# Copies and additions of weight sums spread over the projection tiles of a decoder block, and a later load of token blocks

## The chip, the core and the metric

The kernel runs on one NeuronCore of a Trainium2 chip. The core's engines work side by side, each through its own list of instructions in order: TensorE (PE in the profile, with its weight loads as PEld), VectorE (DVE), ScalarE (ACT), GpSimd (POOL) and SyncE (SP), which here only issues DMA transfers. Sixteen DMA engines carry the transfers of all queues. The metric is the device time of one launch in microseconds, the median of several runs.

## What is computed

One decoder block over 1040 positions (16 learned meta tokens and 1024 tokens) of width 1024, in float32:

```python
h = layer_norm(concat(meta, x))
p = h @ w_in + b_in            # u_s5 | q | k | v | o | i | f | g_s5 | g_m
y_s5 = glu(gelu(s5(u_s5)) @ s5_w_glu)                  # grouped diagonal state-space model
y_m  = (sigmoid(o) * head_norm(mlstm(silu(conv(q, k)), v, i, f))) @ m_w_out   # 4 heads
mix  = sigmoid(g_s5) * y_s5 + sigmoid(g_m) * y_m
h = layer_norm(alpha * h + mix @ w_o)
h = layer_norm(alpha * h + relu(h @ w_up + b_up)**2 @ w_down)
out = h[:, 16:]
```

## The kernel before

A float32 product is made of three matmuls over operands that are split into a high and a low part (`mm3`, L226 to L228). ACT writes the high part (`whi`, L212) and DVE the low part (`wlo`, L213).

**Stages.** The start (`ln0_pipe`) normalises nine blocks of x, transposes them on PE (L1259) and makes the first four projection tiles; `hT_hi` and `hT_lo` are the split result, and `h_dr` a copy of it in DRAM. Then 42 weight tiles ("jobs") follow, one after the other: `ORDER` lists 30 of them, and a q stands for a q and a k tile, so that tiles 0 to 33 are projections (tile 4 is `v0`, tile 5 the k or q behind it); tiles 34 to 41 are `z0` to `z7`, the tiles of the gated S5 product. Beside them generators in "lanes" run the convolutions, the four mLSTM heads, S5, and at the end `ah_scale` and `up_early`, which prepare later stages (`wpre` tiles, stored to `wu_dr`). A clock of estimated times decides when a lane's next piece is written into the program; a scheduler then orders each engine's list by its own simulated times.

**The first mLSTM head.** `gates` transposes the gate values on PE (tiles `gps`, L375 to L421), stores two rows to DRAM (`grow_dr`, L411, and `wrow_dr`), and each head loads them back spread over all partitions (`gB`, `wiB`, L426 and L428). DVE and ACT turn `gB` into weights (L444, L448), ACT makes `kw` (L460), and PE multiplies (`pu`, L477).

**Seven products.** Behind the tiles, `Seven` computes six gate tiles and the mLSTM's output projection with seven products for a 2 x 2 block of tiles instead of eight. It needs sums of weight blocks, made ahead of it in DRAM by `w_sums`: `ws_dr[p, 0..3]` for three pairs of tiles of `wf` and four of `wmo`. Each transfer covers all pairs of one kind (3 x 256 KB or 4 x 256 KB); GpSimd issues it, and an addition (`accum_op`) adds the source to what stands in DRAM. The lane `ws` issues 11 for each weight, one per 6 us of the estimated clock, from the end of the start on. `Seven` also needs sums of token blocks: `begin` loads four raw blocks (`rawb`, two transfers each) from `h_dr`, and `first` loads its first weights, splits them, and subtracts the blocks (L1000). `begin` is called ahead of `z6`, `first` ahead of `z7`, and `run7` behind all tiles.

**Buffers.** Weights, sums, raw blocks and most temporaries share 30 buffers (`slot`); a new tile waits for the release of the buffer that it takes. SP issues weight loads two tiles ahead of their use (`load_w`, L198).

Of the kernel before, what the change touches and what calls it, by code (L numbers as in the profile page):

```python
# [9 lines left out]
F32 = mybir.dt.float32  # L10
# [3 lines left out]
OP = mybir.AluOpType  # L14
# [19 lines left out]
JU, JQ, JK, JO, JGS, JGM = 0, 4, 8, 12, 20, 28  # L34
# [8 lines left out]
NM = 2  # L43
# [69 lines left out]
def decoder_block(  # L113
# [5 lines left out]
    v_, a_, g_, t_ = nc.vector, nc.scalar, nc.gpsimd, nc.tensor  # L119
    const = ctx.enter_context(tc.tile_pool(name="const", bufs=1, side="left"))  # L120
# [17 lines left out]
    def f32(ap):  # L138
        return ap.bitcast(F32)
# [4 lines left out]
    lanes = {"ml": Lane(), "cv": Lane(), "s5": Lane(), "s5c": Lane(), "s5g": Lane(), "ah": Lane()}  # L144
# [49 lines left out]
    def load_w(job):  # L194
        job.raw = []
        for src, n in job.loads:
            r = slot("wraw") if ring[0] is None else ring[0].tile([P, 1024], F32, tag="wr", bufs=3, name="wraw")
            nc.sync.dma_start(r[:, :n], src)  # L198
            job.raw.append(r)

    def split_w(job, later=False):
        if later:
            return split_now(job, True)
        with tc.high_priority(offset=SPLIT_UP):
            split_now(job)
# [26 lines left out]
    def next_split(jobs, i):  # L232
        if i + 1 < len(jobs) and jobs[i + 1].w is None:
            split_w(jobs[i + 1])
# [721 lines left out]
    ws_dr = dram.tile([7, 4, P, 512], F32, name="ws_dr")  # L956

    def w_sums():
        for n0, p0, w, i0 in ((3, 0, wf, JGM + NM), (4, 3, wmo, 0)):
            def src(r, kh):  # L960
                return bass.AP(tensor=w.tensor, offset=w.offset + (i0 + r) * KT * P * P + 512 * kh,
                               ap=[[2 * KT * P * P, n0], [KT * P, P], [1, 512]])
            a11, a12, a21, a22 = src(0, 0), src(0, 1), src(1, 0), src(1, 1)
            todo = [(0, a21), (2, a11), (1, a21), (3, a12), (0, a22), (2, a21), (1, a22), (3, a21), (1, a11), (3, a22),
                    (3, a11)]
            for i, (s, a) in enumerate(todo):
                d = ws_dr[p0:p0 + n0, s]
                if i < 4:
                    g_.dma_start(d, a)
                else:  # L970
                    g_.dma_start(d, a, accum_op=OP.add)
                yield 6.0

    def home(kh, ch):
        s = (slice(None), slice(4 * kh, 4 * kh + 4), slice(META + 512 * ch, META + 512 * ch + 512))
# [391 lines left out]
    def ah_scale():  # L1367
        gb = [slot("gB0"), slot("bB0")]
        for i in range(2):
            nc.sync.dma_start(gb[i][:, :D], row_bcast(ln0r, D, i * D))  # L1370
        rs = {}
        for t in range(9):
            if t < 8:
                rs[t] = slot("ahr")
                nc.sync.dma_start(rs[t][:, :D], ah0_dr[t * P:(t + 1) * P, :])
            if t == 0:
                yield 4.0
                for i in range(2):
                    v_.tensor_scalar(gb[i][:, :D], gb[i][:, :D], ALPHA, None, op0=OP.mult)
                yield 2.0  # L1380
                continue
            r = rs.pop(t - 1)
            for i, op in enumerate((OP.mult, OP.add)):
                v_.tensor_tensor(r[:, :D], r[:, :D], gb[i][:, :D], op=op)
                yield 1.5
            nc.sync.dma_start(ah_dr[(t - 1) * P:t * P, :], r[:, :D])
# [11 lines left out]
    def up_early():  # L1398
        for p in range(PRE):
            r = [slot("wur"), slot("wur")]  # L1400
            for j in range(2):
                nc.sync.dma_start(r[j][:, :D], wup[2 * p + j].rearrange("p k f -> p (k f)"))
            yield 3.0
            a11, a12, a21, a22 = r[0][:, 0:512], r[0][:, 512:1024], r[1][:, 0:512], r[1][:, 512:1024]
            n1, n2 = wsums(a11, a12, a21, a22)
            yield 3.0
            for n, w in ((1, a11), (2, a12), (3, n2[:, 0:512]), (4, a22), (5, n1[:, 0:512]), (6, n1[:, 512:1024]),
                         (7, a21)):
                o = slot("wpre", F32R)
                a_.activation(o[:, 0:512], w, AF.Copy)  # L1410
                v_.tensor_tensor(o[:, 512:1024], w, f32(o[:, 0:512]), op=OP.subtract)
                nc.sync.dma_start(wu_dr[p, n - 1], f32(o[:, 0:1024]))
                yield 0.9

    for w in ORDER.split():
        n, i = w[0], int(w[1:])
# [22 lines left out]
    for w in LOAD0.split():  # L1439
        i = int(w[1])  # L1440
# [20 lines left out]
    nc.sync.dma_start(bupt, bup)  # L1461

    jobs = all_jobs
    lanes["ws"] = Lane()
    lanes["ws"].add(w_sums())
    begin, first, run7 = gates_and_output()

    for i, j in enumerate(jobs):
        if j.raw is None and j.w is None:
            load_w(j)  # L1470
        if j.w is None:
            split_w(j)
        if j.ran:
            next_split(jobs, i)
        for d in (1, 2):
            if i + d < len(jobs) and jobs[i + d].raw is None and jobs[i + d].w is None:
                load_w(jobs[i + d])
        if j.tag == S5_START:
            lanes["s5c"].add(s5_pre())
        if j.tag and j.tag[0] == "o":  # L1480
            while int(j.tag[1:]) not in HMREADY:
                lanes["cv"].drain()
                lanes["ml"].step()
        if j.tag == "g4":
            lanes["ah"].add(ah_scale())
            lanes["ah"].add(up_early())
        if j.tag == "z6":
            mid_ctx.close()
            ring_ctx = ExitStack()
            ring[0] = ring_ctx.enter_context(tc.tile_pool(name="ring", bufs=1, side="left"))  # L1490
            begin()
        if j.tag == "z7":
            first()
        j.run(j)
        j.w = None

    for l in lanes.values():
        l.drain()
    run7()
    ring_ctx.close()  # L1500

# [405 lines left out]
    todo = [(0, 1), (1, 1), (0, 2), (2, 1), (1, 2), (2, 2)] + [(p, n) for n in (6, 7, 5, 4, 3) for p in range(PRE)]  # L1907
# [164 lines left out]
```

## Time and profile before

| | |
|---|---|
| median of 3 runs | 1590.44 us (1588.78 to 1593.2) |
| profiled execution | 1586.42 us, span 1584.1 us |
| mean granted TensorE clock | 0.979 |
| DMA | 266.91 MB, mean 168 GB/s |
| q1 (SP's transfers) | 234.18 MB, 44.1% of 16 engines' span |
| q0 (GpSimd's transfers) | 31.43 MB, 9.0% |
| weight sums | 22 transfers of 768 KB or 1024 KB, all issued in the first 185 us |

All times within the run are microseconds from the start of the span. A profile's row of waits names the engine and line that sat idle and what ended that; a row of a stretch gives the busy time of every engine in it. An idle engine costs time only where the end of the program hangs on it. The granted clock is TensorE's; 1.00 is full speed.

### The profile page before, as it was taken

What the parts mean: (1) busy time and instruction counts of PE and PEld (TensorE: products, weight loads), DVE (VectorE), ACT (ScalarE), POOL (GpSimd) and SP (SyncE); (2) the same over time, 40 slices, a digit from 0 to 9 for tenths busy, and PEclk for the clock granted to TensorE, in tenths of its full rate; (3) what the DMA queues carried; (4) which work ended last, traced back from release to release, by engine and by line L of the source; (5) the groups of instructions that cost most, each with busy time, mean ns of one, the idle gap of its engine ahead of it and who ended that gap; (6) DMA issues with size and microseconds to landing.
All of it is one profiled execution on the core that took longest, in us unless ns stands there. A gap on an engine that the chain in (4) does not pass through costs nothing.

```text
span 1584.1 us, 20491 instructions
## 1 busy us (share of the span) xinstructions
PE 1513.0 (96%) x7593; PEld 1276.8 (81%) x7593; DVE 1078.4 (68%) x2083; ACT 643.7 (41%) x982; POOL 62.2 (4%) x121
## 2 busy tenths in 40 slices
PE   7969699999899999989999999999999999999997
PEld 6968599899787878868788888888888888888886
DVE  6456465567876855666879675766666769775876
ACT  5413244433545433325635224544444534433340
POOL 3121100000000000000000001000000000000000
PEclk8979799999999999999999999999999999999999
DMA  9987641230432157674344217734443698667642
GB/s 320 277 165 145 136 93 41 97 94 22 122 94 68 53 191 271 218 285 170 116 146 160 101 60 221 250 141 148 151 157 135 211 371 318 235 220 235 224 170 107
DMA packets 156803, 266.91 MB, mean 168 GB/s; under 512 B 46920, under 2 KB 68880, under 8 KB 156704
## 3 DMA queue, kind: packets, MB, share of 16 engines
q1 hardware_dynamic: 116464, 234.18, 44.1%
q0 software_dynamic: 40240, 31.43, 9.0%
q8 instruction: 59, 0.97, 0.2%
q14 instruction: 40, 0.33, 0.1%
HBM read 194.29 MB, written 90.05 MB: 179 GB/s over the span
## 4 chain that ended last, share of the span: by engine, by line
PE 70%; issue 16%; DMA 7%; DVE 4%; ACT 2%; SPq 1%; POOLq 0%; ACTq 0%; DVEq 0%
PE mm L226 17%; PE mm L228 17%; PE mm L227 17%; PE sd L226 3%; PE sd L227 3%; PE sd L228 3%; PE mm L1303 1%; DMA gB<-grow_dr 1%; DMA wraw<-in_wv_dram 1%; DMA wraw<-in_wf_dram 1%; DMA wu_dr<-wpre 1%; PE pu L477 1%; DMA wur<-in_wup_dram 1%; PE pn L473 1%; PE mm L1311 1%
## 5 line engine op out<-in xcount | busy, mean ns | idle before, releaser
L226 PE MATMUL mm<-hT_hi,whi 128*128 128x512 f32 (+3 forms) x604 | 228.5, 378 | 1.4 <-ACT whi L212 1.4
L227 PE MATMUL mm<-hT_lo,whi 128*128 128x512 f32 (+3 forms) x604 | 226.7, 375 | 0.0
L228 PE MATMUL mm<-hT_hi,wlo 128*128 128x512 f32 (+3 forms) x604 | 225.0, 377 | 0.1
L226 PEld LDWEIGHTS mm<-hT_hi,whi 128*128 128x128 f32 x604 | 113.5, 188 | 19.4 <-ACT whi L212 1.8
L227 PEld LDWEIGHTS mm<-hT_lo,whi 128*128 128x128 f32 x604 | 113.6, 188 | 18.2 <-issue 0.7
L228 PEld LDWEIGHTS mm<-hT_hi,wlo 128*128 128x128 f32 x604 | 113.5, 188 | 18.2 <-DVE wlo L1041 0.5
L227 PE MATMUL sd<-dwl,dah 128*128 128x512 f32 x240 | 94.5, 394 | 0.0
L226 PE MATMUL sd<-dwh,dah 128*128 128x512 f32 x240 | 94.2, 393 | 0.0
L228 PE MATMUL sd<-dwh,dal 128*128 128x512 f32 x240 | 94.1, 393 | 0.0
L1771 ACT ACTIVATE dwh<-wdr 128x1024 fp32r<-128x1024 f32 x56 | 58.9, 1054 | 85.7 <-DMA wdr<-in_wdn_dram 29.3
L1767 ACT ACTIVATE dah<-da 128x1024 fp32r<-128x1024 f32 x56 | 58.7, 1052 | 84.7 <-PE sd L227 38.2
L213 DVE TENSOR_TENSOR wlo<-wraw,whi 128x1024 fp32r<-128x1024 f32 (+1 forms) x46 | 56.1, 1220 | 49.8 <-DMA wraw<-in_wf_dram 24.3
L226 PE MATMUL mm<-dwh,dah 128*128 128x512 f32 (+1 forms) x224 | 84.6, 378 | 0.0
L227 PE MATMUL mm<-dwl,dah 128*128 128x512 f32 (+1 forms) x224 | 84.5, 378 | 0.0
L228 PE MATMUL mm<-dwh,dal 128*128 128x512 f32 (+1 forms) x224 | 84.4, 377 | 0.0
L1768 DVE TENSOR_TENSOR dal<-da,dah 128x1024 fp32r<-128x1024 f32 x56 | 68.2, 1219 | 21.6 <-ACT dah L1767 21.6
L226 PE MATMUL mm<-whi,hT_hi 128*128 128x256 f32 (+1 forms) x256 | 76.4, 299 | 4.2 <-DVE v L354 3.5
L1772 DVE TENSOR_TENSOR dwl<-wdr,dwh 128x1024 fp32r<-128x1024 f32 x56 | 68.2, 1219 | 13.4 <-ACT dwh L1771 12.8
L228 PE MATMUL mm<-whi,hT_lo 128*128 128x256 f32 (+1 forms) x256 | 75.2, 294 | 0.0
L227 PE MATMUL mm<-wlo,hT_hi 128*128 128x256 f32 (+1 forms) x256 | 74.7, 292 | 0.0
L228 PE MATMUL mm<-th,wul 128*128 128x512 f32 x156 | 61.6, 395 | 0.0
L226 PE MATMUL mm<-th,wuh 128*128 128x512 f32 x156 | 61.6, 395 | 0.0
(473 smaller groups left out, 3663.4 us busy)
## 6 DMA issues: line engine op xcount, KB each, us to landing
da<-act_dr SPq DMA_DIRECT2D x56, 512.0 KB, 5.6
wdr<-in_wdn_dram SPq DMA_DIRECT2D x56, 512.0 KB, 6.4
wur<-in_wup_dram SPq DMA_DIRECT2D x32, 512.0 KB, 4.4
act_dr<-upy SPq DMA_DIRECT2D x64, 256.0 KB, 2.4
wraw<-in_wf_dram SPq DMA_DIRECT2D x30, 512.0 KB, 5.3
ws_dr<-in_wmo_dram POOLq DMA_DIRECT2D x11, 1024.0 KB, 29.4
wu_dr<-wpre SPq DMA_DIRECT2D x21, 512.0 KB, 5.6
wpre<-wu_dr POOLq DMA_DIRECT2D x21, 512.0 KB, 5.2
```

The costliest lines, as they stand in the source:

```text
L213: todo.append(lambda e=v_, r=r, hi=hi, lo=lo, n=n: e.tensor_tensor(lo[:, :n], r[:, :n], f32(hi[:, :n]), op=OP.subtract))
L226: t_.matmul(ps, ah, bh, start=(i == 0 and part[0]), stop=False, skip_group_check=skip)
L227: t_.matmul(ps, ah, bl, start=False, stop=False, skip_group_check=skip)
L228: t_.matmul(ps, al, bh, start=False, stop=(i == n - 1 and part[1]), skip_group_check=skip)
L473: t_.matmul(pn[:, :257], qi[:, c0:c0 + n], Cs[c][:, :257], start=True, stop=False)
L477: t_.matmul(pu[:, :257], kws[c][:n], vt[c][:n, :257], start=True, stop=True)
L1303: t_.matmul(acc[w][:, :c1 - c0], jobs[i].w[0][a][:, k * P:(k + 1) * P], (hT_hi, hT_lo)[b][:, k, c0:c1], start=(first and k == 0), stop=(la ...
L1311: t_.matmul(ps, raw[i][:, k * P:(k + 1) * P], hf(0, k)[:, t * P:(t + 1) * P], start=(k == 0), stop=(k == KT - 1), skip_group_check=True)
L1767: a_.activation(ah[:, :D], a[:, :D], AF.Copy)
L1768: v_.tensor_tensor(alo[:, :D], a[:, :D], f32(ah[:, :D]), op=OP.subtract)
L1771: a_.activation(wh, raw[i], AF.Copy)
L1772: v_.tensor_tensor(wl, raw[i], f32(wh), op=OP.subtract)
```

## The change

`w_sums` now makes the sums with 8 transfers for each weight. Of the four sums two are first copied into another place in DRAM and then extended (`d[1] <- d[0]`, `d[3] <- d[1]`). The transfers leave the estimated clock: from tile 5 on, ahead of every second tile, one is written into the program. Ahead of each stands a copy of one element of that tile's split weights into `mark`, on GpSimd too, so that the transfer isn't issued before the split. The last of 16 goes with tile 35, `z1`. `begin` moves from `z6` to `z7`, and `first` from `z7` to behind all tiles and lanes.

```diff
     def w_sums():
-        for n0, p0, w, i0 in ((3, 0, wf, JGM + NM), (4, 3, wmo, 0)):
+        todo = {}
+        for s, (n0, p0, w, i0) in enumerate(((3, 0, wf, JGM + NM), (4, 3, wmo, 0))):
...
-            todo = [(0, a21), (2, a11), (1, a21), (3, a12), (0, a22), (2, a21), (1, a22), (3, a21), (1, a11), (3, a22),
-                    (3, a11)]
-            for i, (s, a) in enumerate(todo):
-                d = ws_dr[p0:p0 + n0, s]
-                if i < 4:
-                    g_.dma_start(d, a)
-                else:
-                    g_.dma_start(d, a, accum_op=OP.add)
-                yield 6.0
+            d = [ws_dr[p0:p0 + n0, i] for i in range(4)]
+            todo[s] = [(d[0], a21, 0), (d[2], a11, 0), (d[0], a22, 1), (d[2], a21, 1), (d[1], d[0], 0), (d[1], a11, 1),
+                       (d[3], d[1], 0), (d[3], a12, 1)]
+        mark = const.tile([1, 1], F32, name="mark")
+        for s, i in ((0, 0), (0, 1), (0, 2), (0, 3), (0, 4), (1, 0), (0, 5), (1, 1), (0, 6), (1, 2), (0, 7), (1, 3),
+                     (1, 4), (1, 5), (1, 6), (1, 7)):
+            job = yield
+            g_.tensor_copy(mark, f32(job.w[0][0][0:1, 0:1]))
+            d, a, add = todo[s][i]
+            tc.keep_in_program_order(g_.dma_start(d, a, accum_op=OP.add) if add else g_.dma_start(d, a))
...
-    lanes["ws"] = Lane()
-    lanes["ws"].add(w_sums())
+    ws = w_sums()
+    next(ws)
...
-        if j.tag == "z6":
+        if j.tag == "z7":
             mid_ctx.close()
...
             begin()
-        if j.tag == "z7":
-            first()
+        if i >= 5 and i % 2 and ws:
+            try:
+                ws.send(j)
+            except StopIteration:
+                ws = None
         j.run(j)
         j.w = None
 
     for l in lanes.values():
         l.drain()
+    first()
     run7()
```

How the instructions then stand on the engines, at three places. GpSimd's list at the start, before (`meta_hl` holds the meta tokens' columns for the value tiles, `v` the column of ones of the values):

```order
L336 MEMSET v_878 16x1
L969 DMA ws_dr<-in_wf_dram 3x128x512 x4
L336 MEMSET v_1411 16x1
L969 DMA ws_dr<-in_wmo_dram 4x128x512 x4
L971 DMA ws_dr<-in_wf_dram 3x128x512 x4
L1456 CAST meta_hl<-hT_hi 128x8x16
L971 DMA ws_dr<-in_wmo_dram 4x128x512
L1457 CAST meta_hl<-hT_lo 128x8x16
L971 DMA ws_dr<-in_wmo_dram 4x128x512 x3
```

and now:

```order
L336 MEMSET v_879 16x1
L336 MEMSET v_1409 16x1
L1458 CAST meta_hl<-hT_hi 128x8x16
L1459 CAST meta_hl<-hT_lo 128x8x16
L336 MEMSET v_880 128x1 x4
L972 COPY mark<-whi 1x1
L974 DMA ws_dr<-in_wf_dram 3x128x512
L336 MEMSET v_881 128x1 x4
L972 COPY mark<-whi 1x1
L974 DMA ws_dr<-in_wf_dram 3x128x512
```

The sums have left the start of the list; the casts stand ahead of all of them, and each transfer stands behind a `mark`.

PE's list around the second group of the gates' transposes (`gps`), before, where they stand behind the meta tokens' products of the tile `v1`:

```order
L227 MATMUL mm<-hT_lo,whi 128x400
L228 MATMUL mm<-hT_hi,wlo 128x400
L340 MATMUL mm<-whi,meta_hl 48x256 x8
L344 MATMUL mm<-wlo,meta_hl 16x256 x8
L392 MATMUL gps<-ident,gts 1x36
L393 MATMUL gps<-ident,gts 1x36
L394 MATMUL gps<-ident,gts 128x36
L226 MATMUL mm<-whi,hT_hi 128x256
```

and now, where they stand in the first block of the tile ahead of `v1`:

```order
L228 MATMUL mm<-hT_hi,wlo 128x400
L226 MATMUL mm<-hT_hi,whi 128x256
L227 MATMUL mm<-hT_lo,whi 128x256
L392 MATMUL gps<-ident,gts 1x36
L393 MATMUL gps<-ident,gts 1x36
L394 MATMUL gps<-ident,gts 128x36
L228 MATMUL mm<-hT_hi,wlo 128x256
L226 MATMUL mm<-hT_hi,whi 128x256
```

They have moved from rows 415 to 417 of PE's list to rows 343 to 345. The product `pu`, the first that needs their result, is row 573 before and row 574 now.

SP's list around `z6` and `z7`, before:

```order
L198 DMA wraw<-in_wglu_dram 128x1024
L1412 DMA wu_dr<-wpre 128x1024 x3
L989 DMA rawb<-h_dr 128x2x512 x2
L1412 DMA wu_dr<-wpre 128x1024 x2
L989 DMA rawb<-h_dr 128x2x512
L1412 DMA wu_dr<-wpre 128x1024
L989 DMA rawb<-h_dr 128x2x512 x5
L1412 DMA wu_dr<-wpre 128x1024
L1022 DMA wraw<-ws_dr 128x512 x6
```

and now:

```order
L1414 DMA wu_dr<-wpre 128x1024
L198 DMA wraw<-in_wglu_dram 128x1024
L1414 DMA wu_dr<-wpre 128x1024 x7
L991 DMA rawb<-h_dr 128x2x512 x8
L1024 DMA wraw<-ws_dr 128x512 x6
```

All raw blocks are now issued behind the last of the seven stores, where before they stood among them.

## The prediction

> **What bounds the kernel now.** I read the page first (busy time and the slices), then PE's waits, then stretches of 20 us where PE was not full, then what ACT, DVE, SP and POOL did there, and last the DMA queues of those stretches.
>
> ```profile
> PE 1513.0 (96%) x7593; PEld 1276.8 (81%) x7593; DVE 1078.4 (68%) x2083; ACT 643.7 (41%) x982; POOL 62.2 (4%) x121
> PE   7969699999899999989999999999999999999997
> DMA  9987641230432157674344217734443698667642
> ```
>
> PE is the bound: 1513.0 of 1584.1 us. So at most some 71 us of idle PE time are to be had, plus what a lowered clock costs behind a wait. The second line puts the low digits at the start, in slices 3 and 5 (40 us each), and hardly anywhere behind slice 18; the third shows the DMA engines near full in just those first slices. PE's waits (engine and line that waited, who ended it, total, count, longest), up to 500 us and, last two rows, from 540 to 860 us:
>
> ```profile
> PE mm L340 <- ACT whi L212: 14.7, 2, 13.1
> PE pu L477 <- ACT kw L460: 11.7, 1, 11.7
> PE ln L1259 <- ACT hf L1273: 4.0, 1, 4.0
> PE ln L1259 <- ACT x L1247: 4.0, 1, 4.0
> PE mm L226 <- DVE v L354: 3.5, 1, 3.5
> PE gps L421 <- ACT gts L418: 2.6, 1, 2.6
> PE mm L1311 <- DMA wraw<-in_wf_dram: 1.4, 1, 1.4
> PE mm L226 <- ACT whi L212: 6.1, 1, 6.1
> PE s5z L802 <- DMA s5U<-us_dr: 2.8, 1, 2.8
> ```
>
> The same as stretches (length; busy us and count of PE, PEld, DVE, ACT, POOL; granted clock; DMA share; GB/s):
>
> ```profile
> 80.00:100.00 20.00, 6.71 (x38) 5.78 (x39) 6.27 (x7) 2.55 (x3) 4.12 (x3) 0.57 0.88 202
> 140.00:160.00 20.00, 16.64 (x126) 15.67 (x125) 9.99 (x42) 4.88 (x8) 4.31 (x3) 1.00 0.72 107
> 160.00:180.00 20.00, 10.35 (x73) 9.93 (x71) 1.88 (x7) 0.21 (x1) 2.12 (x5) 0.82 0.78 145
> 180.00:200.00 20.00, 14.43 (x92) 13.57 (x93) 18.52 (x70) 9.77 (x15) 2.48 (x14) 0.75 0.63 130
> 680.00:690.00 10.00, 10.00 (x45) 8.16 (x44) 7.45 (x12) 5.01 (x9) 0.00 (x0) 1.00 0.58 223
> 700.00:710.00 10.00, 5.11 (x14) 3.78 (x15) 8.10 (x10) 3.83 (x5) 0.00 (x0) 0.66 1.01 392
> ```
>
> Who was late behind ACT and DVE? Start, length, engine, line, and in brackets the idle time before and what ended it:
>
> ```profile
> 15.20 1.06 ACT L212 ACTIVATE whi<-wraw 128x1024 fp32r<-128x1024 f32 x1 [4.25 <-DMA wraw<-in_wf_dram]
> 90.49 1.08 ACT L212 ACTIVATE whi<-wraw 128x1056 fp32r<-128x1056 f32 x1 [11.36 <-DMA wraw<-in_wv_dram]
> 153.95 0.46 DVE L557 TENSOR_SCALAR s_t<-s_lam 128x16 f32<-128x16 f32 x1 [6.16 <-DMA s_lam<-in_s5l_dram]
> 180.78 1.14 DVE L444 SCALAR_TENSOR_TENSOR gB<-gB,acol,mask 128x128 f32<-128x128 f32 x4 [12.17 <-DMA gB<-grow_dr]
> 701.24 0.63 ACT L1410 ACTIVATE wpre<-wur 128x512 fp32r<-128x512 f32 x1 [10.69 <-DMA wu_dr<-wpre]
> ```
>
> Every one of PE's long waits goes back to a DMA that landed late. Queue q0 is POOL's, and there it carries only the weight sums; q1 is SP's. From 0 to 25 us (rows 1, 2), from 22 to 200 us (3 to 6), and the same loads later, without weight sums beside them (200 to 400 us, 400 to 560 us):
>
> ```profile
> q1 hardware_dynamic: 2106, 5.63, 62.4%
> q0 software_dynamic: 2905, 2.72, 32.5%
> q0 software_dynamic: 34441, 18.38, 56.4%
> q1 hardware_dynamic: 11667, 15.96, 28.3%
> wraw<-in_wv_dram SPq DMA_DIRECT2D x2, 528.0 KB, 19.1
> gB<-grow_dr SPq DMA_DIRECT2D x1, 512.0 KB, 19.1
> gB<-grow_dr SPq DMA_DIRECT2D x2, 512.0 KB, 5.9
> wraw<-in_wf_dram SPq DMA_DIRECT2D x11, 512.0 KB, 4.5
> ```
>
> The weight sums took twice as much of the 16 engines as all loads and stores (56.4% against 28.3%), and 512 KB landed in 19.1 us beside them, in 4.5 to 5.9 us without.
>
> **The change part by part.**
>
> *Start, 0 to 25 us (term A).* Before, the sums start with the kernel; after, none is issued before tile 5, counted from 0. If the engines give SP's queue the 32.5% as well, its bytes need about 62.4/(62.4+32.5) = 0.66 of the time, and W1, which ACT waits for until 15.20, lands near 10. The two waits of 4.0 us and a further 1.4 us for weights are all there is: between 0 and 9.4 us. The first wait is half ACT's own work, so I take 5.
>
> *First value tile, 78 to 97 us (term B).* The two loads behind the 14.7 us land 13 us sooner if they take 4.5 to 5.9 us. SP issues them at 70 to 75 us, though, since buffers come free only then:
>
> ```profile
> 70.30 5.32 SPq L198 DMA_DIRECT2D wraw<-in_wv_dram x2
> ```
>
> The second goes out at about 73, lands near 79, and its split ends near 81, just behind PE's products of the first: 1.5 us are left of the wait. The clock of 0.57 cost at most 0.43 x 6.71 = 2.9 us more; I take 2. Sum 14.7 - 1.5 + 2 = 15. Lowest 8 (SP's own stores are still in the way: they are part of the 28.3%), highest 17.
>
> *Start of the first mLSTM head, 140 to 200 us (term C).* Waits 2.6 + 3.5 + 11.7 = 17.8 us, and a clock of 0.82 and 0.75, at most 0.18 x 10.35 + 0.25 x 14.43 = 5.5 us, of which I take 4. Between the gates' transposes and `pu`, some 5 us behind the DVE row at 180.78, lie 40 us with three late DMAs: s_lam (6.16 us of DVE's wait), gB (19.1) and, from the chain that ended last,
>
> ```profile
> 155.66 5.54 DMA grow_dr<-gts
> 132.32 0.28 PE L226 MATMUL mm<-hT_hi,whi 128*128 128x256 f32 x1
> 145.70 0.19 PE L392 MATMUL gps<-ident,gts 36*1 36x36 f32 x1
> ```
>
> If all three fall as gB did, to 5.9/19.1, they give back 4 + 13 + 4 us and the chain takes 19. The order moves these transposes 72 rows forward on PE, to where PE stood at 132 (row 2; row 3 is where they were), while `pu` stays (row 573, now 574). Between the two PE had 40 - 17.8 = 22 us of work and now has 13 more: 35 us cover a chain of 19, and would cover it with gB at 19. What is late next is DVE: its 36.7 us in the four rows from 80 and 140 us fall into about 48, three quarters full, and it frees PE's banks in order. I leave 3 us: 17.8 + 4 - 3 = 19 (10 to 22).
>
> *Six transfers fewer; a `mark` copy ahead of each.* The sums fall from 14 additions and 8 copies to 8 and 8. Sixteen copies of one element cost POOL, 4% busy, nothing that anyone waits for: a `mark` reads a split that is done a tile ahead, and an addition waits for a transfer issued four tiles earlier, but for the last three. Zero, with up to 3 us of loss if POOL, waiting there, is late with S5's memsets (L723, L753, L764), which stand behind in its queue.
>
> *The sums beside the rest of the projections (term E).* This is the price of the change. Tile 4 starts near 91 us and z7, tile 41, near 699, so tiles 5 to 35 lie at about 100 to 600 us, 33 us a pair. No trace of before has a sum there, but this one shows the ingredients: two late sums on POOL, and from 175 to 200 us the last one's landing, the queue's share and weight loads beside it.
>
> ```profile
> 164.69 1.92 POOL L971 DMA_DIRECT2D ws_dr<-in_wf_dram x1 [10.28 <-DMA ws_dr<-in_wf_dram]
> 181.47 1.89 POOL L971 DMA_DIRECT2D ws_dr<-in_wmo_dram x1 [14.66 <-DMA wraw<-in_wf_dram]
> ws_dr<-in_wmo_dram POOLq DMA_DIRECT2D x1, 1024.0 KB, 29.8
> q0 software_dynamic: 3585, 1.72, 43.5%
> wraw<-in_wf_dram SPq DMA_DIRECT2D x3, 512.0 KB, 13.9
> ```
>
> With no more than two sums in flight q0 held 43.5% of 16 engines, 7, and still one took 29.8 us. So a sum alone takes between 9 us (if it quickens as gB did) and 30 (if it keeps to 3 or 4 engines); the share is nearer the second. Then a sum is under way most of the time, and a load that uses all engines waits for the slowest. Weights are loaded two tiles ahead and can take 13.9 us. Exposed are chains that PE waits for: gB of three more heads, S5's blocks (2.8 us already). Bounds: 0 (all covered) and 20 (three heads, each at half of gB's 13 us). With half as many sums in flight and slack as in term C, I take 6 lost.
>
> The Trainium skill speaks against the change here: DMA: Bandwidth & Descriptors, in its section on why a DMA increments its semaphore by 16, says that a transfer runs on the largest number of engines up to 16 that divides the slowest dimension of both sides, which is 3 and 4 for these; 7 for two agrees. By that rule a sum alone stays near 30 us and E is 6, as taken; by the other reading, 9 us, E would be 2 and the time 1547.
>
> *Raw blocks one tile later (term D).* PE's 6.1 us at 699 is z7's split on ACT, which stands behind a `wpre` that waited 10.69 us for a store to land. Before, eight raw loads stand between those stores; now all seven stores come first. The wait is then covered, and with 1.5 us of clock (0.34 x 5.11 = 1.7 at most) 7.6 us go. Late next: seven stores and eight raw loads of 512 KB, 7.9 MB, need 20 us at the 392 GB/s of that row; the first stores were out when the `wpre` began to wait at 690.5, so the raw blocks have landed by about 709. DVE's subtractions of them now stand ahead of the low half of the gates' first weight tile, which PE needs behind z7's 48 products, at 699 + 11 = 710 (45 products in 10 us in the row of 680). I leave 1.6: gain 6 (from -3 to 7.6).
>
> Sum: 5 + 15 + 19 + 6 - 6 = 39. The profiled execution took 1586.42 us (span 1584.1), so 1547.4; the median of the runs, 1590.44, stands 4.0 higher, so 1551.
>
> **The rivals.**
>
> *Half lost to contention (0.18).* The sums hold engines through the projections and every head pays. For: 13.9 us for weights beside two sums. Against: weights come two tiles ahead. With E at -20, 1565; with C at 12 as well, 1572. The Trainium skill's DMA: Bandwidth & Descriptors, Queues, rings and completion order, has each engine take turns between queues packet by packet; by that one sum is enough to halve a load on the engines they share, and this rival is the result.
>
> *A new wait at the gates' sums (0.10).* The raw blocks come after all stores, DVE stands at a subtraction, the split behind it is late: D is -3 to -6, in all 1560 to 1563. For: 392 GB/s at 700. Against: by the 20 us above they are just in time.
>
> *Slower (0.05).* One mechanism: sums in flight without pause from 100 to 620 us make gB land in 19.1 us for heads 1 to 3 too, and each stalls PE as head 0 did, by 17.8 us and 2 of clock: 59 us against a gain of 45, 1604. It decides once more than 2.3 heads pay in full. Against: chain C has 16 us of slack once its DMAs are early, and 512 KB took 13.9 beside two sums.
>
> *It does nothing (0.04).* SP's own stores make the loads late: 1590. Against: q1 has half of q0's share.
>
> **How the numbers follow.** My sum has 0.60, 1539 to 1562, which is all terms two thirds of the way to their upper bounds (17 us in all) or a quarter of the way to their lower ones (44 us); 0.03 is for more (1534 with every term at its upper bound). The range, 1539 to 1573, takes in the first, the raw blocks' rival and most of the contention. Within 0.3% (5 us, about what this measurement can tell from no change) is the last rival, 0.04; slower 0.05; faster 0.91.
>
> **What would show it.** A and B: PE's waits at L1259 and L340 shrink to under 6 and 2 us, and the value loads land in 6 to 9. C: none at `pu`, gB's DVE wait under 6. E: waits from 200 to 560 us grow by no more than 10, q0 near 15% there. D: no `wpre` wait behind a store, no PE wait near z7 above 2 us. I am wrong if head 1's `pu` or S5's products wait instead, or if DVE holds PE from 100 to 200 us.

## The result: 1579.6 us, and the profile after

| kernel | median us | ratio to before | 95% interval |
|---|---|---|---|
| before | 1590.6 (1588.8 to 1593.2) | | |
| changed | 1579.6 (lowest 1577.9) | 0.9926 | 0.9907 to 0.9946 |

One of the changed kernel's four executions took 5692.6 us at a granted clock of 0.258; the ratio leaves it out, and the median of the other three is 1579.1.

The change won 0.74%, some 11 us. I had forecast 1551 and a range of 1539 to 1573, so the time lies above the range. The profiled execution of the changed kernel took 1577.87 us, its span is 1576.1 us, 8.0 less than before.

The page of the changed kernel, busy time, PE's slices and those of the DMA engines:

```profile
PE 1516.2 (96%) x7593; PEld 1278.9 (81%) x7593; DVE 1079.4 (68%) x2083; ACT 642.8 (41%) x982; POOL 70.2 (4%) x131
PE   8999999998899798999999999999999999999997
DMA  8412324414344466685344317744443799667642
```

The 6 of PE in slices 3 and 5 (39 us each) is a 9 now, and the DMA engines' 9, 8, 7 and 6 in slices 2 to 5 are 4, 1, 2 and 3. New low digits of PE stand in slices 10, 14 and 16, between 355 and 630 us, the lowest, 7, at 512 to 552. PE's waits of the changed kernel, of the first 500 us (the five longest and `pu`), then the five longest of 500 to 860 us:

```profile
PE s5z L802 <- DMA s5U<-us_dr: 5.7, 1, 5.7
PE s5y L858 <- DVE s5w L846: 4.8, 2, 4.3
PE ln L1261 <- ACT x L1249: 3.7, 1, 3.7
PE gps L421 <- ACT gts L418: 1.8, 1, 1.8
PE pt L513 <- DVE hraw L506: 1.7, 1, 1.7
...
PE pu L477 <- ACT kw L460: 1.4, 1, 1.4
```

```profile
PE s5z L802 <- DMA s5U<-us_dr: 9.6, 1, 9.6
PE mm L227 <- DVE gell L878: 7.0, 1, 7.0
PE mm L228 <- DVE wlo L1043: 3.9, 2, 2.8
PE mm L226 <- ACT whi L212: 2.1, 2, 1.4
PE mm L228 <- DVE wlo L213: 1.6, 4, 0.5
```

The 14.7 us at the first value tile and the 11.7 at `pu` have gone, as forecast. In their place stand S5's products (5.7 and 9.6 us, both for `s5U`, 2.8 before), the gated product's first low half (`gell`, 7.0) and the splits behind it.

To see where the time went, take the moment at which the same instruction starts on PE in each trace. "Lead" is how much earlier than before it starts; the last column is the difference of the spans. The places are the first `pu` (185.57 us before), S5's first output products (407.13), its second and fourth batch's first products `s5z` (429.89, 559.85), and z0's first product (621.11). The kernels below the first line are those of the experiments.

| lead, us | `pu` | S5 out | `s5z` 2 | `s5z` 4 | z0 | end |
|---|---|---|---|---|---|---|
| changed | 37.8 | 38.4 | 31.5 | 22.4 | 20.6 | 8.0 |
| e_none (no sums' traffic) | 41.1 | 43.2 | 43.6 | 42.3 | 40.9 | 49.1 |
| e_spread (wide) | 40.3 | 40.9 | 40.4 | 39.3 | 39.5 | 45.4 |
| e_pad | 37.2 | 39.4 | 33.4 | 24.2 | 22.0 | 6.6 |
| e_last3 | 37.5 | 38.0 | 31.0 | 21.3 | 19.9 | 27.3 |
| e_latewide | 38.4 | 40.6 | 38.3 | 37.4 | 35.9 | 43.2 |
| e_copywide | 41.8 | 43.9 | 44.6 | 43.2 | 41.8 | 35.9 |
| e_dense | 38.1 | 36.0 | 24.3 | 20.3 | 18.9 | 27.7 |
| b_spread | -11.7 | -9.8 | -8.7 | -9.5 | -11.1 | -12.5 |
| b_tail | 1.8 | 1.4 | 0.5 | -0.1 | -1.7 | 3.3 |
| s_tail | 40.5 | 41.1 | 40.8 | 40.1 | 40.2 | 40.7 |
| s_dense | 42.0 | 44.1 | 45.2 | 44.5 | 43.0 | 49.3 |
| s_22 | 42.1 | 44.2 | 42.6 | 41.5 | 40.0 | 47.7 |

Up to 407 us the changed kernel had won 38.4 us. It loses 17.8 of them between there and z0, and 12.6 more from z0 to the end.

What S5's chain waits for is seen in SP's queue. Its issues from 514 to 536 us in the changed kernel (start, length of the issue, line, transfer), and SP's waits of 500 to 535 us:

```profile
514.88 10.82 SPq L758 DMA_DIRECT2D s5Mx<-s5Kt  x16
532.71 2.20 SPq L786 DMA_DIRECT2D s5U<-us_dr  x5
```

```profile
SPq L758 <- DVE s5Kt L745: 12.8, 1, 12.8
SPq L786 <- DMA s5Mx<-s5Kt: 7.0, 1, 7.0
SPq L786 <- PE s5z L802: 3.5, 1, 3.5
```

Sixteen small transfers of `s5Mx` went out by 525.7; SP then stood 7.0 us until some of them had landed, and only then issued the last five of `s5U`. GpSimd's list and the landing times of 515 to 545 us say what lay beside them:

```profile
519.95 0.61 POOL L974 DMA_DIRECT2D ws_dr<-ws_dr  x1 [0.36 <-issue]
ws_dr<-ws_dr POOLq DMA_DIRECT2D x1, 12.6
s5Mx<-s5Kt SPq DMA_DIRECT2D x2, 8.0 KB, 10.0
```

The copy within `ws_dr` was under way from 520 to 532.5 us, and beside it transfers of 8 KB took 10 us. SP went on in the moment when the copy landed.

### The profile page after: what moved, and what is told of

It reads as the page before. It is cut to its first block, busy times and chain, and to the rows that moved or that the text cites. A ratio compares the mean times of both kernels' runs of the same rounds, so it can differ in the third digit from the quotient of the medians.

```text
span 1576.1 us, 20513 instructions
## 1 busy us (share of the span) xinstructions
PE 1516.2 (96%) x7593; PEld 1278.9 (81%) x7593; DVE 1079.4 (68%) x2083; ACT 642.8 (41%) x982; POOL 70.2 (4%) x131
## 4 chain that ended last, share of the span: by engine, by line
PE 39%; issue 15%; DMA 2%; DVE 1%; ACT 0%; SPq 0%; POOLq 0%; DVEq 0%; ACTq 0%
PE mm L228 10%; PE mm L227 9%; PE mm L226 9%; PE sd L227 3%; PE sd L226 3%; PE sd L228 3%; DMA wur<-in_wup_dram 1%; DMA wu_dr<-wpre 1%; DMA rawb<-h_dr 1%; PE ln L1565 0%; DVE rawb L1002 0%; DVE wpre L1413 0%; DVE sgs L945 0%; DVE z2s L944 0%; DVE wlo L1043 0%
## 5 line engine op out<-in xcount | busy, mean ns | idle before, releaser
L1773 ACT ACTIVATE dah<-da 128x1024 fp32r<-128x1024 f32 x56 | 58.7, 1051 | 84.8 <-PE sd L227 37.8
L1778 DVE TENSOR_TENSOR dwl<-wdr,dwh 128x1024 fp32r<-128x1024 f32 x56 | 68.2, 1220 | 12.4 <-ACT dwh L1777 11.8
L213 DVE TENSOR_TENSOR wlo<-wraw,whi 128x1024 fp32r<-128x1024 f32 (+1 forms) x46 | 56.1, 1223 | 18.0 <-ACT whi L212 15.2
L227 PE MATMUL mm<-tl,wuh 128*128 128x512 f32 x156 | 61.5, 394 | 0.0
```

The source lines that it names most:

```text
L213: todo.append(lambda e=v_, r=r, hi=hi, lo=lo, n=n: e.tensor_tensor(lo[:, :n], r[:, :n], f32(hi[:, :n]), op=OP.subtract))
L227: t_.matmul(ps, ah, bl, start=False, stop=False, skip_group_check=skip)
L1773: a_.activation(ah[:, :D], a[:, :D], AF.Copy)
L1778: v_.tensor_tensor(wl, raw[i], f32(wh), op=OP.subtract)
```

## Experiments

Ratios are to the kernel before, measured with each group on the same chip; their 95% intervals stand behind them. The groups ran on different chips, so kernels of two groups are better compared by their ratios than by their microseconds (0.001 is 1.6 us). In the first group the question is what it is in a sum that delays S5: large pieces, few engines, or neither.

### e_pad: rows of 2 KB instead of pieces of 64 KB

```diff
-    ws_dr = dram.tile([7, 4, P, 512], F32, name="ws_dr")
+    ws_dr = dram.tile([7, 4, P, 528], F32, name="ws_dr")
-            d = [ws_dr[p0:p0 + n0, i] for i in range(4)]
+            d = [ws_dr[p0:p0 + n0, i, :, 0:512] for i in range(4)]
-                    a = ws_dr[self.p0 + p, s]
+                    a = ws_dr[self.p0 + p, s, :, 0:512]
```

> The changed kernel (median 1579.6 us), with 16 unused columns behind each row of ws_dr, so that the four copies within ws_dr can't run as 64-KB pieces any more and go row by row (2 KB), like all the other sums; every engine's list is unchanged. Theory 'large pieces': the two copies at 384 and 520 us hold S5's small transfers, that stand in SP's queue, until a 64-KB piece is through; with 2-KB pieces the two PE waits for s5U (5.7 us at 398, 9.6 at 537) fall to at most 1 and 3, and the time to 1564 to 1570. Theory 'few engines': it is that a sum holds 3 or 4 engines, whatever the pieces; both waits stay within 1.5 us of what they were and the time stays at 1577 to 1582. Theory 'other': the waits go and the time stays, since something behind them is as late (PE's wait for gell at 616).

Measured: 1578.7 us, 0.9935 (0.9915 to 0.9955): no change that can be told from nothing. PE's waits of this kernel for S5, of 350 to 460 us and of 460 to 600 us:

```profile
PE s5z L802 <- DMA s5U<-us_dr: 4.8, 1, 4.8
PE s5z L802 <- DMA ys_dr<-s5Y: 8.9, 1, 8.9
```

4.8 and 8.9 us in place of 5.7 and 9.6 (the second row names a store that was under way beside `s5U`). SP's own wait behind `s5Mx` fell to 3.0 us and `s5U` was issued from 526.31 on instead of 532.71, but then took 7.3 us to land instead of 2.5. The copy of 1024 KB took 14.8. So "large pieces", a theory of mine when this ran, fell as the cause of the lost time.

### e_spread: the same bytes over 128 rows

The 128 rows become the slowest dimension of both sides, where 3 or 4 pairs were it.

```diff
-                               ap=[[2 * KT * P * P, n0], [KT * P, P], [1, 512]])
+                               ap=[[KT * P, P], [2 * KT * P * P, n0], [1, 512]])
-            d = [ws_dr[p0:p0 + n0, i] for i in range(4)]
+            d = [ws_dr[p0:p0 + n0, i].rearrange("n p f -> p n f") for i in range(4)]
```

> The changed kernel, with the 128 rows as the slowest dimension of both sides of all 16 transfers of sums in place of the 3 or 4 pairs: the same bytes in the same 2-KB rows (the copies within ws_dr too), the lists of the engines unchanged. Lone additions took 25 to 28 us for 768 KB and a plain copy 13.4. If these are the times of 3 or 4 engines, a sum now lands in 5 to 10 us and no S5 transfer waits for one: by 'large pieces' and by 'few engines' alike 1560 to 1570, by 'few engines' alone with a clear gain over the padded kernel, by 'large pieces' alone the same as that within 4 us. If a sum spread over 16 engines delays the loads more than before, PE's waits from 200 to 600 us grow over the 21 us of the changed kernel and the time is over 1582.

Measured: 1539.4 us, 0.9684 (0.9662 to 0.9707), some 39 us under the changed kernel (38.5 by the ratios, 40.2 by the medians), with every engine's list but the shape of GpSimd's transfers the same. It is more than I had expected by any theory. The width itself is read from queue q0's share of the 16 engines. From 90 to 125 us one copy of 768 KB runs alone in that queue; first the changed kernel, then this one (packets, MB, share; landing time):

```profile
q0 software_dynamic: 1040, 0.79, 7.1%
ws_dr<-in_wf_dram POOLq DMA_DIRECT2D x1, 768.0 KB, 13.4
```

```profile
q0 software_dynamic: 208, 0.79, 7.7%
ws_dr<-in_wf_dram POOLq DMA_DIRECT2D x1, 768.0 KB, 5.3
```

7.1% of 16 engines over 35 us are 39.8 us of one engine, in 13.4 us: 3.0 engines, one for each pair. 7.7% are 43.1, in 5.3 us: 8.1 on average, start and landing included. The sum costs the engines nearly the same in both; what differs is for how long it holds how many. Counted from the packets' starts and lengths in the two traces, exactly three packets of q0 are under way for 8.7 us of that narrow copy, exactly four for 10.6 us of the one of four pairs at 520 us, and in the wide copy the most frequent count is 16. A 768 KB copy of three pairs and a 1024 KB copy of four took 12.5 and 12.6 us in the changed kernel, as they should if each pair has its engine. The Trainium skill's rule on the number of engines (DMA: Bandwidth & Descriptors, the section on why a DMA increments its semaphore by 16), the largest up to 16 that divides the slowest dimension of both sides, gives 3 and 4 there and 16 here; the packet counts agree. The packets' size doesn't explain it: the copy at 384 us has 80 packets in the changed kernel, fewer than the 208 of the wide one, and takes 12.6 us, and 15.7 with 1040 in the padded kernel.

PE's waits from 500 to 860 us are then

```profile
PE s5z L802 <- DMA s5U<-us_dr: 3.0, 1, 3.0
PE mm L228 <- DVE wlo L1043: 2.3, 1, 2.3
PE s5y L858 <- DVE s5w L846: 1.2, 1, 1.2
```

6.5 us, where the changed kernel has 26.0 in seven groups.

### e_none: no traffic for the sums at all

The transfers move 64 bytes per pair, and `Seven` loads a plain block of weights in place of each sum. It leaves out the sums themselves, so that its output isn't the block's.

```diff
-                               ap=[[2 * KT * P * P, n0], [KT * P, P], [1, 512]])
+                               ap=[[2 * KT * P * P, n0], [KT * P, 1], [1, 16]])
-            d = [ws_dr[p0:p0 + n0, i] for i in range(4)]
+            d = [ws_dr[p0:p0 + n0, i, 0:1, 0:16] for i in range(4)]
-                    a = ws_dr[self.p0 + p, s]
+                    a = self.w[self.i0 + 2 * p].rearrange("p k f -> p (k f)")[:, 0:512]
```

> The changed kernel without the traffic of the sums: each of the 16 transfers moves 64 bytes per pair, and the seven products load a plain block of weights where they would load a sum, so that the gates and the output projection come from other weights. This bounds all that the sums cost beside the rest of the projections. By my own account of the traces (38 us won by 407 us, 28 lost behind that, most of it to sums) it gives 1552 to 1560; if the order of DVE's and ACT's work or the later raw blocks lose the 28 us, it stays over 1570.

Measured: 1536.5 us, 0.9675 (0.9655 to 0.9694). So the narrow sums, placed as the change places them, cost some 40 us (39.9 by the ratios, 41.1 by the spans, 43.1 by the medians of two chips), and all of the time that was missing against the forecast is theirs. I had expected 28 and counted from 407 us on; 5 more lie ahead of that (the leads 43.2 and 38.4), and the gain of the later raw blocks comes out only where no narrow sum runs beside them (next run). Spread wide, the sums cost at most 3, which the intervals don't tell from nothing.

### b_tail: the later raw blocks alone

```diff
-        if j.tag == "z6":
+        if j.tag == "z7":
             mid_ctx.close()
...
             begin()
-        if j.tag == "z7":
-            first()
...
+    first()
     run7()
```

> The kernel before (1590.6) with the later raw blocks alone: begin at z7, first behind all tiles, the sums as before. The prediction's term: 6 us won, 1584 (1583 to 1593). The rival that it gave, a new wait of the gates' first weights behind DVE's subtractions: 1589 to 1594. By the two traces, where a wait of 6.1 us at z7 went and 3.9 us at the gates' weights came: about 1588.

Measured: 1583.9 us, 0.9967 (0.9950 to 0.9983), 4.6 us won, and the lead grows by 5.0 between z0 and the end. That is the forecast's term D, not the rival's. PE's waits of 600 to 760 us are this one row, where before 6.1 us stood behind z7's split:

```profile
PE mm L228 <- DVE wlo L1041: 2.2, 1, 2.2
```

### s_tail: the wide sums with the raw blocks at their old place

The edit of b_tail, backwards, in e_spread.

> The kernel with wide sums (1539.4) and the raw blocks loaded where they were before (begin at z6, first at z7). By the run with the later raw blocks alone, which won 4.6 us, this one is 4 to 7 us slower: 1543 to 1547, with the split of z7 waiting again. If the place of the raw blocks is worth nothing once the sums are out of the way: 1538 to 1541. If the wait of 2.3 us for the gates' first low half is its price: 1535 to 1538.

Measured: 1545.5 us, 0.9718 (0.9698 to 0.9739), 6.1 more than with the later blocks (5.4 by the ratios), and the wait is back:

```profile
PE mm L226 <- ACT whi L212: 5.8, 1, 5.8
```

Both ways of asking give 5 to 6 us for D. In the changed kernel itself it is hidden under the losses of the same stretch.

### b_spread: wide sums at their old place

```diff
-                               ap=[[2 * KT * P * P, n0], [KT * P, P], [1, 512]])
+                               ap=[[KT * P, P], [2 * KT * P * P, n0], [1, 512]])
-                d = ws_dr[p0:p0 + n0, s]
+                d = ws_dr[p0:p0 + n0, s].rearrange("n p f -> p n f")
```

> The kernel before (1588.5 in the last runs) with one edit: the 128 rows are the slowest dimension of both sides of all 22 transfers of sums; they still start with the kernel and are out by 185 us. Theory 'width': what a sum costs others is the time that a load waits for the 3 or 4 engines that the sum holds, and the engines' own time for its bytes matters little. Then most of the 38 us that the changed kernel won by 407 us are won here too, without any move: 1555 to 1568. Theory 'time of the engines': the sums' bytes are the cost (q0 held 56% of 16 engines from 22 to 200 us, and a lone sum takes the same 40 to 85 engine-microseconds in either layout), so that the move was needed: 1578 to 1592, with PE's waits at the value tile and at pu still over 8 us each.

Measured: 1598.9 us, 1.0055 (1.0038 to 1.0071): slower than before. Both theories had put it lower, and of the two waits that the second expected one is there, at 40 us, and the other, at `pu`, is not. PE's longest wait of the first 200 us, the value loads that end it, and the queues from 60 to 135 us:

```profile
PE mm L340 <- ACT whi L212: 40.5, 2, 39.6
wraw<-in_wv_dram SPq DMA_DIRECT2D x2, 528.0 KB, 21.5
q0 software_dynamic: 4791, 9.48, 68.1%
q1 hardware_dynamic: 6121, 8.99, 37.5%
```

One behind the other from the start, the wide sums took 68.1% of the engines in this stretch, where the narrow ones had taken 56.0%. SP issues the two value loads at 94 and 109 us in place of 70 and 75, behind stores that are late too, and the value tile stands 40 us in place of 14.7. Behind it nothing waits at `pu`, so that 10 of the 40 are the net loss at 200 us. The move out of the start was needed, and so was the width: neither does alone what both do.

### e_latewide and e_last3: where the narrow sums cost

Of the 16 transfers the last eight (issued from 384 us on), or the last three (552, 589 and 620 us), are wide, the others narrow.

```diff
+            def wide(ap):
+                return ap.rearrange("n p f -> p n f")
...
+            for i in range(6 - 4 * s, 8):                  # e_latewide
+            for i in (range(0), range(5, 8))[s]:           # e_last3
+                todo[s][i] = (wide(todo[s][i][0]), wide(todo[s][i][1]), todo[s][i][2])
```

> The changed kernel with its first eight sums (issued up to 352 us) narrow as they are, and the last eight (from 384 us on) over 128 rows. Theory 'exposed chains': nearly all of the 40 us between the changed kernel (1579.6) and the one with wide sums (1539.4) comes back: 1541 to 1546. If every narrow sum costs the same: 1557 to 1562. If the first eight hold most of it: over 1565.

> The changed kernel with only its last three sums (issued at 552, 589 and 620 us) over 128 rows, the other 13 narrow. The changed kernel takes 975.6 us from z0's first product to the end, the one with all sums wide 957.0, and between the last batch's S5 products and z0 the former loses 2 more. If the sums under way at that place are the cause, this gives 1579.6 - 18.6 - 2 = 1559 (1556 to 1562), with PE's waits for gell, whi and wlo behind 600 us under 4 us together and the two for s5U (5.7 and 9.6) as they were. If the S5 waits upstream bring the late gell with them: 1568 to 1580.

Measured: 1542.9 us, 0.9708 (0.9681 to 0.9736), and 1556.9 us, 0.9794 (0.9764 to 0.9823). Eight narrow sums, issued up to 352 us, cost 3.5 us against e_spread, which the intervals don't tell from nothing; the last three alone cost some 21 (0.9926 less 0.9794, of 1590). In e_last3 the two waits for `s5U` are as they were (5.5 and 10.1), and from z0 to the end it takes 955.6 us, as little as e_none (954.8; the changed kernel 975.6). So the late `gell` wasn't brought by S5's earlier waits.

What the last three delay shows in the changed kernel's landing times of 575 to 640 us, below them those of e_spread at the same place (550 to 620 us):

```profile
ws_dr<-in_wmo_dram POOLq DMA_DIRECT2D x1, 1024.0 KB, 34.8
ys_dr<-s5Y SPq DMA_DIRECT2D x1, 512.0 KB, 12.1
s5yc<-ys_dr SPq DMA_DIRECT2D x8, 64.0 KB, 8.7
```

```profile
ws_dr<-in_wmo_dram POOLq DMA_DIRECT2D x1, 1024.0 KB, 12.5
ys_dr<-s5Y SPq DMA_DIRECT2D x1, 512.0 KB, 7.0
s5yc<-ys_dr SPq DMA_DIRECT2D x8, 64.0 KB, 4.9
```

The last S5 batch goes through DRAM (`ys_dr`, then `s5yc`) before its gelu: 12.1 + 8.7 us against 7.0 + 4.9. Behind the gelu comes `gell` on DVE, which stands in its list behind `ah_scale`'s multiplications. In the changed kernel these waited too, for a load that stands behind `s5yc` in SP's list:

```profile
607.58 1.23 DVE L1386 TENSOR_TENSOR ahr<-ahr,gB 128x1024 f32<-128x1024 f32 x1 [12.26 <-DMA ahr<-ah_dr]
607.64 1.06 ACT L877 ACTIVATE gelh<-gelf 128x1024 fp32r<-128x1024 f32 x1
615.02 1.22 DVE L878 TENSOR_TENSOR gell<-gelf,gelh 128x1024 fp32r<-128x1024 f32 x1
616.30 0.79 PE L227 MATMUL mm<-gell,whi 128*128 128x512 f32 x1 [7.04 <-DVE gell L878]
```

The gelu's part, `gelh`, was ready at 608.7. DVE then worked off six of those multiplications, from 607.6 to 615.0, before it came to `gell`. So of PE's 7.0 us some 6 hang on the late load of `ah_scale` and on DVE's order, and not on the gelu.

### e_copywide: copies wide, additions narrow

```diff
+            for i in (0, 1, 4, 6):
+                todo[s][i] = (wide(todo[s][i][0]), wide(todo[s][i][1]), todo[s][i][2])
```

> The changed kernel with its eight copies over 128 rows (5 to 7 us each in place of 13) and its eight additions narrow (25 to 37 us) as they are. The S5 batches whose s5U came late stood beside copies within ws_dr (384 and 520 us). Theory 'whatever narrow transfer is under way when a chain loads': those two waits shrink to at most 1 and 3 us, the additions at 552 and 620 still hold the last batch and the gated tiles: 1562 to 1569. If only the additions matter, being the long ones: 1574 to 1581, with both s5U waits as before. If only the copies matter: under 1550.

Measured: 1551.1 us, 0.9757 (0.9728 to 0.9786), lower than expected. The `s5U` waits are gone (none, and 2.7), as said; what I had too high is the end: from z0 on it takes 968.8 us, 11.8 over e_spread and not 18. So 6.8 of the 18.6 us lost there went with the copies, the one at 589 us beside the last batch among them. The additions, 25 to 35 us long, cost the other 12, all of it behind z0; ahead of it the lead is that of the kernel without sums. Why they pass S5 by, whether by their place or by their kind, wasn't tried.

### e_dense: narrow sums, one ahead of every tile

```diff
-        if i >= 5 and i % 2 and ws:
+        if i >= 5 and ws:
```

> The changed kernel with its narrow sums (3 or 4 engines), one ahead of every tile from tile 5 on in place of every second one, so that they are under way without pause from about 95 to 430 us, beside the mLSTM heads, and gone in S5's last two batches and behind. Theory 'exposed chains': narrow sums cost nothing where the chains beside them have slack (150 to 400 us: the lead stayed at 38.4 there) and much where S5 and the gated tiles load late (28 us): 1550 to 1560. The prediction's rival 'slower', in which gB of heads 1 to 3 lands late beside sums without pause: over 1585, with waits at pu of 10 us and more. Between them: 1560 to 1585, where S5's first two batches pay.

Measured: 1559.2 us, 0.9801 (0.9779 to 0.9823), 20 us better than one per two tiles, with not a byte less. This is the test of the prediction's rival "slower": narrow sums without pause beside the heads. PE's waits of 100 to 200 us:

```profile
PE gps L421 <- ACT gts L418: 2.0, 1, 2.0
PE pu L477 <- ACT kw L460: 1.5, 1, 1.5
PE mm L226 <- DVE mlo L348: 1.2, 1, 1.2
```

and between 200 and 350 us there is none. Heads 1 to 3 pay nothing: the lead is 38.6 us at 192 us (times of the kernel before) and 38.8 at 385. The first head pays about as much as in the changed kernel, since e_none leads by 43.0 and 43.2 there. S5's second batch pays (the lead falls from 36.0 to 24.3), and from z0 on, where no sums are left, it takes 954.2 us, as e_none does (954.8).

### s_dense and s_22: wide sums, one ahead of every tile

s_dense is the edit of e_dense in e_spread. s_22 also takes back the 22 transfers:

```diff
-            todo[s] = [(d[0], a21, 0), (d[2], a11, 0), (d[0], a22, 1), (d[2], a21, 1), (d[1], d[0], 0), (d[1], a11, 1),
-                       (d[3], d[1], 0), (d[3], a12, 1)]
+            todo[s] = [(d[0], a21, 0), (d[2], a11, 0), (d[1], a21, 0), (d[3], a12, 0), (d[0], a22, 1), (d[2], a21, 1),
+                       (d[1], a22, 1), (d[3], a21, 1), (d[1], a11, 1), (d[3], a22, 1), (d[3], a11, 1)]
```

> Wide sums (1539.4 at one per two tiles), one ahead of every tile from tile 5 on, so that all are out by about 330 us. The kernel without the sums' traffic took 1536.5, so at most 3 us are left. If a wide sum beside the gated tiles costs those: 1536 to 1538. If twice as many wide sums beside the first heads cost what the narrow ones there do not: 1541 to 1550, with waits at pu or at the value tiles over 3 us.

> The kernel with wide sums, one per tile from tile 5 on (1537.2), but with the 22 transfers of the kernel before (14 additions, no copy within ws_dr) in place of 16, the last one with tile 26. The prediction put nothing on the six transfers fewer: 1535 to 1540. If additions, which take the engines twice as long as copies, still delay S5's chains or the heads when they are wide: 1542 to 1552, with PE's waits from 350 to 600 us over 12 us.

Measured: 1537.2 us, 0.9667 (0.9632 to 0.9701), and 1538.5 us, 0.9681 (0.9663 to 0.9698). Six transfers fewer are worth nothing that could be told apart. s_dense is the fastest version with the sums in it, level with the kernel without their traffic (1536.5, 0.9675) and some 41 us under the changed one; against e_spread (0.9684) the intervals overlap.

## Why the prediction was wrong

**A, B, C: the start, the first value tile, the first head (forecast 5 + 15 + 19 = 39).** Right: the lead is 38.4 us at 407 us. By the same instructions on PE it is 5.4 at the end of the start (72 us), 22.3 behind the first value tile (104) and 38.3 behind the first `pu` (192), so A, B and C gave 5.4, 16.9 and 16.0; that the sum came out within 1 us is in part luck, B being 2 over and C 3 under. None of the 14.7 us is left at L340, 1.4 is at `pu`, 4.6 at L1261, and `gB`'s two waits on DVE are 3.1 and 2.6. e_none adds that the narrow sums still cost some 4 or 5 us here (43.2), all of it in the first head. The five kernels whose first copies are narrow lead by 38.0 to 40.6 us ahead of S5 (e_dense by 38.8), the five with wide ones by 40.9 to 44.2; one trace differs from the next by up to 2.6 us where the program so far is the same (e_last3 and e_latewide).

**D: raw blocks one tile later (forecast 6).** The size was right: 5 to 6 us in b_tail and s_tail. What was to show it in the changed kernel didn't: `wpre` still waits for stores there, 9.6 us in three, and PE waits 3.9 and 1.6 us for low halves. That looked like the rival "a new wait at the gates' sums", but in e_spread it is one wait of 2.3 us on PE, and `wpre` waits 3.0 us for a store: the late narrow sums caused the rest.

**F: fewer transfers and the `mark` copies (forecast 0).** The fewer transfers are right by s_22, among wide sums. No run took the `mark` copies out alone. No engine's wait names them, but the late memset that I had allowed for did come: ACT stands 6.6 us in two waits for POOL's L723, 4.7 in e_none, and never before the change. No wait of PE is put down to POOL. In e_none the lead falls by 2.3 us from 407 us to z0; whether that is the price of the `mark` copies stays open.

**E: the sums beside the rest of the projections (forecast -6, bounds 0 and -20).** This is the step that failed. Its price by the leads, with D put at 5.5: 17.8 us from 407 us to z0, and 12.6 + 5.5 = 18.1 behind, 35.9 in all. Against e_none, by the spans, it is 41.1 less the 4.8 ahead of 407 us, 36.3: 15.5 up to z0 and 20.8 behind.

Two things in the step were right: that a lone sum would keep to 3 or 4 engines, for 25 to 37 us in an addition (a copy took 13), and that q0 would hold some 15% (12.3% from 200 to 560 us).

The bound was wrong in its choice of the payer. I priced it as three more heads at half of `gB`'s delay. Those heads paid nothing, even with narrow sums beside them without pause (e_dense). Who paid were chains with several transfers in a row. Up to z0 it was S5's `us_dr` to `s5U`, with its small `s5Mx` in front of that in SP's queue: PE waited 15.3 us for `s5U`, 2.8 in e_none, and the granted clock around these waits was 0.73 and 0.66 (390 to 400 and 530 to 545 us), in e_none 1.00 and 0.89 (378 to 388 and 508 to 523). Behind 560 us it was `ys_dr` to `s5yc`, `ah_scale`'s loads behind these in SP's list, and `gell` behind `ah_scale` on DVE; PE's waits from z0 to 860 us add up to 15.2 us, 1.5 in e_none. That each transfer of such a chain waits for the slowest of its engines is argued; the runs show that the waits go when the sums are wide.

The profile of before had the row to see it by, 2.8 us of PE's wait at `s5U`, with no slack at all; I quoted it and put no price on it. My last line even named waiting S5 products as a sign of being wrong, and that sign came. And the working counted sums up to 600 us. The lone row that it used, 29.8 us of one landing, says that a sum stays long after its issue: the last of 16 was issued at 620 and landed at 655, beside the gated tiles.

So the rival "half lost to contention" had the cause, sums that hold engines, but not the payers, since every head was to pay and three of four paid nothing; its price for E, 20 us, was little more than half. What I missed is that beside these tiles a sum's cost to others went with the time for which it held its engines, not with its bytes: the same bytes over 16 engines cost at most some 3 us. Where sums run back to back from the start, b_spread shows that this doesn't hold.

## What to carry to other kernels

A background transfer has a width, and it can be read from a profile: its queue's share of the engines, times the stretch, by the landing time. Look at it before placing the transfer in time, since here the slowest dimension's size was worth more (some 39 us) than where the transfers stood (11 us), though only the two together pay: wide transfers all issued at the start made it slower by 0.55%. And price contention at the chains that already wait in the profile of before, and at those that go through DRAM more than once, not at the chain that was slow in the place from which the load is moved away.

## What the runs showed of the hardware beyond that

- Small transfers pay too: beside a copy on four engines, `s5Mx` transfers of 8 KB landed in 10.0 us and those of 4 KB in 9.0; beside the wide one in 2.4 and 1.8. The Trainium skill's rule that an engine takes turns between queues packet by packet (DMA: Bandwidth & Descriptors, Queues, rings and completion order) allows for a delay on the shared engines; which engines they shared, no trace here shows.
- SP's list can stand still for its own late transfers: its wait of 7.0 us ahead of `s5U` in the changed kernel ended with the landing of `s5Mx`. Whether a buffer or something else ties the one to the other, no run here shows.
- The size of the pieces in the copies within `ws_dr` made no difference to the time of the kernel: 1579.6 us with 64 KB, 1578.7 with 2 KB. It moved the delay: the `s5Mx` transfers of 8 KB landed in 6.9 us in place of 10.0, and `s5U` in 7.3 in place of 2.5.
